# Gate and up products of a decoder layer on one NeuronCore: one weight sum as an accumulating transfer, a new order of the weight preparation, and six wide products in 17 blocks

## The chip, the core and the metric

The kernel runs on one core of one Trainium2 chip. The metric is the device time of one execution in microseconds (us); the figure of a kernel is the median of its runs. A profile is one further execution, recorded by the hardware profiler.

## The reference

The reference is one layer of a decoder in float32, with 512 tokens of width 1024: a mixer sublayer (causal stick-breaking attention beside a gated short convolution), cross-attention into 256 memory tokens, and a SwiGLU sublayer with 2816 hidden units, with a final norm. The change touches the first half of the last sublayer alone:

```python
hf = rms_norm(x, norm_ffn[l])
gate, up = jnp.split(hf @ w_ffn_in[l], 2, axis=-1)
x = x + (jax.nn.silu(gate) * up) @ w_ffn_out[l]
```

Here `hf` is 512 x 1024 and `w_ffn_in` is 1024 x 5632.

## The kernel before

**Precision.** TensorE works in a shortened float32 (`F32R`). Each operand is therefore split into a high part, which is a cast by ScalarE (`nc.scalar.copy`), and a rest, which is a subtraction on VectorE (`rest_of`, L1006). A product of two operands is three matmuls: high by high, high by rest, rest by high.

**Blocks and products.** The hidden units are worked in `NF` = 22 blocks of 128. A block needs a 1024 x 128 gate part and a 1024 x 128 up part of the weights. Pairs of row blocks of the activations against pairs of weight columns make 2 x 2 block products, and these are computed in a form that needs seven products instead of eight, of sums and differences of the operands. The tokens stand in two halves of `HS` = 256 columns. So a block has seven products, numbered 0 to 6, each over `KP` = 4 steps of 128 rows. The sums and differences of the activations (`forms_of`, L697) are made once, in the residual stage ahead. The activation forms of products 1, 2, 5 and 6 lie side by side, high half and rest half, in one tile of 512 columns (`both` in `product`); those of 3 and 4 are made the same way, but only their two halves are handed on.

**Narrow and wide products** (`product`, L899). A narrow product takes three matmuls of 256 columns per step, 12 in all, into the left half of a PSUM bank. A wide product takes, per step, one matmul of 512 columns (the weights' high part against both halves) and, after all four steps, one of 256 columns per step (the weights' rest against the high half): 4 and 4. The right half of its bank then holds a part that has to be added later. Products 1, 2 and 6 are wide in all blocks, product 5 in blocks 5 to 18 (`WIDE`, L921).

**Banks.** Products 0, 3, 4 and 5 of a block add up in one bank `z`, and ScalarE copies intermediate states out of it (`reads`, L939) to the tiles `s` and `t`. Product 1 goes to bank `v`. Products 2 and 6 add up in bank `y`. VectorE joins the two halves of a wide bank with an older state in two additions of 256 columns (`joined_halves`, L935): after product 1 and after product 6 for the gate, and in `second` for product 2. `evict` (L955) scales the gate, applies Silu on ScalarE and multiplies by the up part.

**The weights of a block.** Four quarters of 256 KB lie in HBM. `ffn_load` (L846) loads one quarter twice into `ws` and two quarters into `wg`, both through SP's queue, and then adds two quarters onto `ws` by an accumulating transfer of 512 KB through POOL's queue (L862). `sum_third` (L872) adds one half of `ws` onto `wg` on VectorE; `sum_last` (L876) adds the two halves of `wg` on VectorE and writes into the second half of a further tile `a22`, whose first half `load_corner` (L865) has filled with a quarter from HBM. `pair_cast` casts two forms at once: `wg` for products 0 and 1 (number 0), `ws` for products 4 and 2 (number 1), `a22` for products 5 and 6 (number 2). `third_cast` casts the form of product 3. Casts go to the tags `wh` and `wl`, four buffers each; `ws` and `wg` take turns over three blocks.

**The order.** PE, ScalarE and VectorE run a hand-written order. `uses` lists the products; from block 2 on the row of a block m is:

```python
uses += [(m, 3), (m, 2), (m, 4), (m + 1, 0), (m + 1, 1), (m, 5), (m, 6)]
```

The table `todo` (filled by `at` and `made`, L1076 and L1080) tells which casts, rests, sums and transfers are issued behind which product; `made` issues a cast at one place and its rest on VectorE at the next. ScalarE and VectorE work through their instructions in that order. SP and POOL only issue transfers here and are not in the manual order; each still issues its own in order.

Of the kernel before, what the change touches and what calls it, by code (L numbers as in the profile page):

```python
# [13 lines left out]
P = 128  # L14
# [12 lines left out]
HS = S // 2  # L27
# [17 lines left out]
def hybrid_layer(ctx: ExitStack, tc: tile.TileContext, xT_d, memT_d, mem_d, cols_d, wv_d, win_d,  # L45
# [653 lines left out]
    def forms_of(xe, xo):  # L699
# [144 lines left out]
    KP = KD // 2  # L844
    raws, corners = {}, {}

    def ffn_load(m):
# [4 lines left out]
        s13 = s13[0].tile([P, 2, 512], F32, tag=s13[1], name=nm("ws"))  # L852
        i = nc.sync.dma_start(s13, a[:, 2:3, :].broadcast_to([P, 2, 512]))
        if m < 2:
            after(i, [loads[-6]])
        wg = wg[0].tile([P, 2, 512], F32, tag=wg[1], name=nm("wg"))
        i = nc.sync.dma_start(wg, a[:, 0:2, :])
        if m < 2:
            after(i, [loads[-6]])
        if m < 2:  # L860
            load_corner(m)
        nc.gpsimd.dma_start(s13, a[:, 0:4:3, :], accum_op=ALU.add)  # L862
        raws[m] = wg, s13
# [12 lines left out]
    def sum_last(m, eng=nc.vector):  # L876
        wg = raws[m][0]
        eng.tensor_tensor(out=corners[m][:, 1, :], in0=wg[:, 0, :], in1=wg[:, 1, :], op=ALU.add)
# [22 lines left out]

    def product(ps, m, i, ks=range(KP)):

        rests = []
        for k in ks:
            hi, lo = (w[:, k * P:(k + 1) * P] for w in wforms[m, i])
            xh, xl, *both = x2f[k][i]
            if both and (i != 5 or m in WIDE):
                nc.tensor.matmul(ps, hi, both[0], start=i < 3 and k == 0, stop=False,  # L909
                                 skip_group_check=True)  # L910
                rests.append((ps[:, :HS], lo, xh))
                continue
            for j, (a, b) in enumerate(((hi, xh), (hi, xl), (lo, xh))):
                nc.tensor.matmul(ps[:, :HS], a, b, start=i < 3 and k == 0 and j == 0,  # L914
                                 stop=k == KP - 1 and j == 2, skip_group_check=True)
        for operands in rests:
            nc.tensor.matmul(*operands, start=False,  # L917
                             stop=ks[-1] == KP - 1 and operands is rests[-1],
                             skip_group_check=True)

    WIDE = range(5, NF - 3)  # L921
    banks, silus = {}, []
# [16 lines left out]
    def reads(m, i):  # L939

        b = banks[m]
        z, s, t = b["z"][:, :HS], b["s"], b["t"]
        if i == 5 and m in WIDE:
            nc.scalar.copy(s[:, :HS], b["z"][:, HS:])
        elif i in (0, 3, 4):
# [3 lines left out]
        elif i == 6:  # L949
            joined_halves(b["g"][:, HS:], b["y"], s[:, HS:])  # L950

    def second(m):
        b = banks[m]
        joined_halves(b["t"][:, HS:], b["y"], b["t"][:, :HS])

    def evict(m, part):
# [6 lines left out]
        else:  # L963
# [5 lines left out]
            if m in WIDE:  # L969
                first = b["s"][:, :HS]  # L970
                nc.vector.tensor_tensor(out=first, in0=b["z"][:, :HS], in1=first, op=ALU.add)
# [8 lines left out]
    uses = [(0, 0), (0, 1), (0, 2), (1, 0), (1, 1), (0, 3), (1, 3), (0, 4), (1, 2), (0, 5), (0, 6),  # L980
            (1, 4), (2, 0), (2, 1), (1, 5), (1, 6)]
    for m in range(2, NF - 1):
        uses += [(m, 3), (m, 2), (m, 4), (m + 1, 0), (m + 1, 1), (m, 5), (m, 6)]
    m = NF - 1
    uses[-1:] = [(m, 3), (m, 2), (m, 4), (m - 1, 6), (m, 5), (m, 6)]
# [153 lines left out]
    for m in range(NF - 2):  # L1139
        at(uses.index((m, 1)), lambda m=m: ffn_load(m + 2))  # L1140
    for m in range(1, NF - 1):
        p = {i: uses.index((m, i)) for i in range(2, 7)}
        q = {i: uses.index((m + 1, i)) for i in range(2)}
        if m > 1:
            at(p[3], lambda m=m: sum_third(m + 1))
# [4 lines left out]
            made(p[2], third_cast, m + 1)  # L1150
        else:
            made(p[4], third_cast, m + 1)
        at(p[4], lambda m=m: second(m))
        if m + 2 < NF:
            at(p[4], lambda m=m: load_corner(m + 2))
        made(q[0], pair_cast, m + 1, 1, late=2)
        at(q[1] if m < NF - 2 else p[4], lambda m=m: sum_last(m + 1))
        if m + 2 < NF:
            made(p[5], pair_cast, m + 2, 0)
# [34 lines left out]
    with tc.manual_schedule(engines={mybir.EngineType.PE, mybir.EngineType.Activation,  # L1194
# [6 lines left out]
        for n, (m, i) in enumerate(uses):  # L1201
            if n == 3:
                product(banks[m]["z"], m, i, range(KP - 1, KP))
            elif n > 3:
                product(bank_of(m, i), m, i)
# [329 lines left out]
```

## Time and profile before

| what | us |
|---|---|
| median of 3 runs | 839.65 |
| lowest and highest of them | 839.28, 840.1 |
| profiled execution | 838.75 |
| its span, first to last instruction | 837.0 |
| first to last product of gate and up | 502.4 to about 721 |

The profile page gives, per engine, busy time, share of the span and count of instructions. PE is TensorE's matmuls, PEld its weight loads, DVE VectorE, ACT ScalarE, POOL GpSimd, SP the engine that issues most transfers. A group of the page reads: line, engine, operation, written tile <- read tiles, shapes, count, then busy time and mean ns of one, then idle time of the engine just before, with what ended it. A row of the timeline reads: start from the span's beginning, length, engine, line, operation, tiles, shape, count of merged instructions. The length of a merged row of matmuls reaches to the end of the last one, which overlaps the next row, so the pace of PE is read from starts. A row on a queue of transfers reads: packets, MB, share of the 16 DMA engines. A row of issues ends in the median time from issue to landing.

### The profile page before, as it was taken

The page shows a single profiled execution, that of the slowest core. Times are in us where ns is not written, and L with a number is a line of the kernel's source. Part 1 is how long each engine was busy: PE and PEld are TensorE (multiplying, and loading weights), DVE is VectorE, ACT ScalarE, POOL GpSimd, SP SyncE. Part 2 cuts the span into 40 slices and gives each one's busy share as a digit, 9 for nine tenths or more (in the row PEclk, how much of TensorE's full clock was granted, in tenths as well). Part 3 has the DMA queues.
Part 4 walks back from the last instruction along what each step waited for, and adds up shares of the span by engine and source line. Part 5 has one row for each costly group of instructions (what it writes and reads, how often), then busy time and mean ns, then how long its engine had stood idle before and what let it go on. Part 6 is the DMA issues. An engine that isn't in the chain of part 4 may idle for free.

```text
span 837.0 us, 11962 instructions
## 1 busy us (share of the span) xinstructions
PE 828.8 (99%) x4374; PEld 714.1 (85%) x4374; DVE 684.6 (82%) x1086; ACT 463.9 (55%) x796; POOL 161.2 (19%) x168
## 2 busy tenths in 40 slices
PE   9999999999999999999999999999999999999996
PEld 7888888888888888888888789999999999888885
DVE  7879899996756576587555698999999999999886
ACT  7567868674332355434444566645555555576654
POOL 0011131110566630173000031111111110000401
PEclk9999999999999999999999999999999999999999
DMA  8552435235687865566431326677767673465552
GB/s 303 155 166 101 122 111 103 74 115 174 228 312 276 304 249 188 182 233 249 148 82 51 101 51 161 167 184 200 197 180 197 176 184 95 170 213 197 180 183 101
DMA packets 51357, 143.69 MB, mean 172 GB/s; under 512 B 5761, under 2 KB 7041, under 8 KB 48482
## 3 DMA queue, kind: packets, MB, share of 16 engines
q1 hardware_dynamic: 41650, 107.89, 38.2%
q0 software_dynamic: 9360, 34.75, 15.8%
q8 instruction: 34, 0.56, 0.3%
q10 hardware_dynamic: 288, 0.28, 0.1%
q14 instruction: 25, 0.20, 0.1%
HBM read 125.20 MB, written 13.64 MB: 166 GB/s over the span
## 4 chain that ended last, share of the span: by engine, by line
PE 99%; DVE 0%; ACT 0%; DVEq 0%; issue 0%
PE z L914 13%; PE p L1228 12%; PE pr L161 8%; PE pr L162 8%; PE pr L163 8%; PE y L909 5%; PE r L162 3%; PE r L163 3%; PE r L161 3%; PE v L288 3%; PE y L917 2%; PE v L909 2%; PE km L666 2%; PE mq L163 2%; PE mq L161 2%; PE mq L162 2%
## 5 line engine op out<-in xcount | busy, mean ns | idle before, releaser
L156 ACT CAST wh<-wr 128x1024 fp32r<-128x1024 f32 x84 | 88.0, 1051 | 144.2 <-issue 80.0
L157 DVE TENSOR_TENSOR wl<-wr,wh 128x1024 fp32r<-128x1024 f32 x84 | 111.0, 1321 | 32.0 <-ACT wh L156 31.9
L161 PE MATMUL pr<-xgh,wh 128*128 128x512 f32 x288 | 112.8, 392 | 0.0
L162 PE MATMUL pr<-xgl,wh 128*128 128x512 f32 x288 | 112.4, 390 | 0.0
L163 PE MATMUL pr<-xgh,wl 128*128 128x512 f32 x288 | 112.3, 390 | 0.0
L611 POOL TENSOR_TENSOR pre<-pre 128x512 f32<-128x512 f32 x44 | 70.9, 1616 | 31.5 <-DMA pre<-in_w_ffn_out_dram 29.2
L862 POOL DMA_DIRECT2D ws<-in_w_ffn_in_dram x22 | 26.6, 1209 | 248.5 <-DVE c L708 54.0
L163 PEld LDWEIGHTS pr<-xgh,wl 128*128 128x128 f32 x288 | 54.1, 188 | 11.5
L161 PEld LDWEIGHTS pr<-xgh,wh 128*128 128x128 f32 x288 | 54.1, 188 | 10.6
L162 PEld LDWEIGHTS pr<-xgl,wh 128*128 128x128 f32 x288 | 54.1, 188 | 10.5
L914 PE MATMUL z<-xd,wf 128*128 128x256 f32 x360 | 47.5, 282 | 0.0
L946 ACT COPY sa<-z 128x256 f32<-128x256 f32 x44 | 16.4, 373 | 51.9 <-PE z L914 51.9
L914 PEld LDWEIGHTS z<-xd,wf 128*128 128x128 f32 x360 | 45.0, 190 | 0.1
L1006 DVE TENSOR_TENSOR wf<-wg,wf 128x1024 fp32r<-128x1024 f32 (+1 forms) x44 | 43.1, 978 | 1.5
L1006 DVE TENSOR_TENSOR wl<-wr,wh 128x1024 fp32r<-128x1024 f32 x33 | 41.0, 1242 | 1.8 <-ACT wh L1073 1.8
L1073 ACT CAST wh<-wr 128x1024 fp32r<-128x1024 f32 x33 | 34.5, 1050 | 5.3 <-ACT f01h L1002 2.6
L914 PE MATMUL z<-xf,wf 128*128 128x256 f32 x264 | 35.4, 283 | 0.0
L914 PE MATMUL z<-xc,wf 128*128 128x256 f32 x264 | 35.1, 283 | 0.0
L914 PEld LDWEIGHTS z<-xf,wf 128*128 128x128 f32 x264 | 33.4, 192 | 0.1
L914 PEld LDWEIGHTS z<-xc,wf 128*128 128x128 f32 x264 | 33.0, 190 | 0.0
L368 DVE TENSOR_TENSOR g<-pr,r0b 128x512 f32<-128x512 f32 x16 | 11.0, 687 | 23.5 <-PE pr L163 23.5
L417 POOL TENSOR_SCALAR_AFFINE_SELECT e<-e 128x128 f32<-128x128 f32 (+1 forms) x24 | 10.7, 447 | 86.6 <-DVE e L470 86.6
(356 smaller groups left out, 2239.9 us busy)
## 6 DMA issues: line engine op xcount, KB each, us to landing
wr<-in_w_in_dram SPq DMA_DIRECT2D x36, 512.0 KB, 3.4
pre<-in_w_ffn_out_dram POOLq DMA_DIRECT2D x11, 1024.0 KB, 8.0
sums<-pre POOLq DMA_DIRECT2D x11, 1024.0 KB, 5.0
ws<-in_w_ffn_in_dram SPq DMA_DIRECT2D x22, 512.0 KB, 4.8
wg<-in_w_ffn_in_dram SPq DMA_DIRECT2D x22, 512.0 KB, 4.7
ws<-in_w_ffn_in_dram POOLq DMA_DIRECT2D x22, 512.0 KB, 5.7
wr<-sums SPq DMA_DIRECT2D x22, 512.0 KB, 4.0
wr<-in_w_ffn_out_dram SPq DMA_DIRECT2D x16, 512.0 KB, 3.7
```

The lines of the kernel that those rows point to most:

```text
L156: after(nc.scalar.copy(h2, raw), lead[-1:])
L157: lows.append(nc.vector.tensor_tensor(out=l2, in0=raw, in1=f(h2), op=ALU.subtract))
L161: nc.tensor.matmul(ps, a[0], b[0], start=start, stop=False, **kw)
L162: nc.tensor.matmul(ps, a[0], b[1], start=False, stop=False, **kw)
L163: nc.tensor.matmul(ps, a[1], b[0], start=False, stop=stop, **kw)
L611: nc.gpsimd.tensor_tensor(out=t[:, a, :], in0=t[:, a, :], in1=t[:, b, :], op=ALU.add)
L862: nc.gpsimd.dma_start(s13, a[:, 0:4:3, :], accum_op=ALU.add)
L909: nc.tensor.matmul(ps, hi, both[0], start=i < 3 and k == 0, stop=False, skip_group_check=True)
L914: nc.tensor.matmul(ps[:, :HS], a, b, start=i < 3 and k == 0 and j == 0, stop=k == KP - 1 and j == 2, skip_group_check=True)
L1006: nc.vector.tensor_tensor(out=lo, in0=src, in1=f(hi), op=ALU.subtract)
L1073: nc.scalar.copy(hi, raw)
L1228: nc.tensor.matmul(res[i][s2], a[:, ts], b, start=j == 0 and n == 0, stop=n == 2 and j == (BEHIND - 1 if (i, s2) == (5, 1) else NJ - 1))
```

## The change

1. Products 3 and 4 hand on their 512-column tiles, and in blocks 3 to 19 (the new `WIDE`, 17 blocks) products 3, 4 and 5 are wide beside 1, 2 and 6. Only product 0 stays narrow there. ScalarE copies all 512 columns of bank `z` after products 3 and 4, and VectorE folds them in with one addition of 512 and one of 256 columns (`folded`) in place of two of 256.
2. Products 5 and 6 of these blocks run as a pair: the eight matmuls of 512 columns of both, then the eight of 256 columns (`beside_next`, `later`).
3. In blocks 4 to 20 (`OWN`) the last sum is no longer VectorE's: POOL issues an accumulating transfer of 256 KB from the first half of `wg` onto its second half. The corner quarter is then loaded over that first half, and `pair_cast` number 2 reads `wg`; `a22` isn't used in these blocks.
4. The order around it moves: the sum of the third form stands behind product 5 of the block two ahead, followed by the accumulating transfer; the third form's cast and the cast for products 0 and 1 come a product earlier; the loads into `ws` are issued earlier than those into `wg`; the corner's load stands behind product 2 of the preceding block.

```diff
-        return [(u[:, a], u[:, b]), first, second, third[:2], fourth[:2], fifth, last]
+        return [(u[:, a], u[:, b]), first, second, third, fourth, fifth, last]
...
+    OWN = range(4, NF - 1)
...
+            after(nc.gpsimd.dma_start(s13, a[:, 0:4:3, :], accum_op=ALU.add), own_sums[-1:])
 
     def load_corner(m):
 
+        if m in OWN:
+            nc.sync.dma_start(raws[m][0][:, 0, :], wfi_d[m][:, 3 * 512:])
+            return
...
     def sum_last(m, eng=nc.vector):
         wg = raws[m][0]
+        if m in OWN:
+            own_sums.append(nc.gpsimd.dma_start(wg[:, 1, :], wg[:, 0, :], accum_op=ALU.add))
+            return
...
-        raw = (*raws[m], corners[m])[which]
+        raw = (*raws[m], raws[m][0] if m in OWN else corners[m])[which]
...
-            if both and (i != 5 or m in WIDE):
+            if both and (i not in (3, 4, 5) or m in WIDE):
...
-    WIDE = range(5, NF - 3)
+        if later:
+            return ends
+        ends()
+
+    WIDE = range(3, NF - 2)
...
-        if i == 5 and m in WIDE:
-            nc.scalar.copy(s[:, :HS], b["z"][:, HS:])
+        if m in WIDE and i in (3, 4):
+            nc.scalar.copy((s, t)[i - 3], b["z"])
+        elif m in WIDE and i == 5:
+            nc.scalar.copy(t[:, :HS], b["z"][:, HS:])
+        elif m in WIDE and i == 6:
+            folded(b["g"][:, HS:], b["y"], s)
...
+    def folded(out_, bank, old):
+        nc.vector.tensor_tensor(out=old, in0=bank, in1=old, op=ALU.add)
+        nc.vector.tensor_tensor(out=out_, in0=old[:, :HS], in1=old[:, HS:], op=ALU.add)
+
     def second(m):
         b = banks[m]
+        if m in WIDE:
+            folded(b["t"][:, HS:], b["y"], b["t"])
+            return
...
+        if m + 2 in OWN:
+            made(q[1], pair_cast, m + 2, 0)
+            at(p[5], lambda m=m: sum_third(m + 2), lambda m=m: sum_last(m + 2))
...
+            elif (m, i) in beside_next:
+                ends = [product(bank_of(*use), *use, later=True) for use in uses[n:n + 2]]
+                ends[0]()
```

In the rows below, each instruction stands with its line, operation, written tile, read tiles and columns; numbers behind names tell buffers apart.

On PE, product 3 of block 5 before, with the start of product 2 behind it (`z_5351` is the block's bank z, `xd` the activation form, `wf` the weights):

```order
L914 MATMUL z_5351<-xd_4436,wf_5331 128x256 x3
L914 MATMUL z_5351<-xd_4537,wf_5331 128x256 x3
L914 MATMUL z_5351<-xd_4638,wf_5331 128x256 x3
L914 MATMUL z_5351<-xd_4739,wf_5331 128x256 x3
L909 MATMUL y_5435<-xc_4430,wf_5369 128x512
```

The same product of the same block now (its bank z is `z_5332`):

```order
L922 MATMUL z_5332<-xd_4436,wf_5302 128x512
L922 MATMUL z_5332<-xd_4537,wf_5302 128x512
L922 MATMUL z_5332<-xd_4638,wf_5302 128x512
L922 MATMUL z_5332<-xd_4739,wf_5302 128x512
L932 MATMUL z_5332<-xd_4436,wf_5302 128x256
L932 MATMUL z_5332<-xd_4537,wf_5302 128x256
L932 MATMUL z_5332<-xd_4638,wf_5302 128x256
L932 MATMUL z_5332<-xd_4739,wf_5302 128x256
```

Twelve matmuls of 256 columns became four of 512 and four of 256.

On PE, product 5 of block 5 and the start of product 6 before (`y_5435` is its bank y):

```order
L909 MATMUL z_5351<-xd_4439,wf_5432 128x512
L909 MATMUL z_5351<-xd_4540,wf_5432 128x512
L909 MATMUL z_5351<-xd_4641,wf_5432 128x512
L909 MATMUL z_5351<-xd_4742,wf_5432 128x512
L917 MATMUL z_5351<-xd_4439,wf_5433 128x256
L917 MATMUL z_5351<-xd_4540,wf_5433 128x256
L917 MATMUL z_5351<-xd_4641,wf_5433 128x256
L917 MATMUL z_5351<-xd_4742,wf_5433 128x256
L909 MATMUL y_5435<-xo_4442,wf_5432 128x512
```

The same place now (bank y is `y_5412`):

```order
L922 MATMUL z_5332<-xd_4439,wf_5409 128x512
L922 MATMUL z_5332<-xd_4540,wf_5409 128x512
L922 MATMUL z_5332<-xd_4641,wf_5409 128x512
L922 MATMUL z_5332<-xd_4742,wf_5409 128x512
L922 MATMUL y_5412<-xo_4442,wf_5409 128x512
L922 MATMUL y_5412<-xo_4543,wf_5409 128x512
L922 MATMUL y_5412<-xo_4644,wf_5409 128x512
L922 MATMUL y_5412<-xo_4745,wf_5409 128x512
L932 MATMUL z_5332<-xd_4439,wf_5410 128x256
```

Product 6 begins ahead of the second half of product 5, four matmuls of 256 columns earlier.

On VectorE, from the join of product 1 of block 9 to the end of block 8's row before (`wg_5617` and `ws_5615` are block 9's, `wg_5733` and `ws_5731` block 10's, `fg_5720` is block 8's gate):

```order
L937 TENSOR_TENSOR fg_5833<-v_5832,fg_5833 128x256
L878 TENSOR_TENSOR a_5692<-wg_5617 128x512
L1006 TENSOR_TENSOR wf_5830<-ws_5615,wf_5829 128x1024
L936 TENSOR_TENSOR fg_5720<-y_5779,sa_5695 128x256
L937 TENSOR_TENSOR fg_5720<-y_5779,fg_5720 128x256
L1006 TENSOR_TENSOR wf_5861<-wg_5733,wf_5860 128x1024
L874 TENSOR_TENSOR wg_5733<-ws_5731,wg_5733 128x512
L960 TENSOR_TENSOR fg_5720<-fg_5720,r0b_4940 128x512
L1006 TENSOR_TENSOR wf_5890<-a_5692,wf_5889 128x1024
L1006 TENSOR_TENSOR wf_5903<-wg_5733,wf_5903 128x512
```

The same place now (`ws_5510` is block 9's, `ws_5614` and `wg_5684` are block 10's, `fg_5673` is block 8's gate):

```order
L956 TENSOR_TENSOR fg_5777<-v_5776,fg_5777 128x256
L1039 TENSOR_TENSOR wf_5774<-ws_5510,wf_5773 128x1024
L1039 TENSOR_TENSOR wf_5791<-wg_5684,wf_5790 128x1024
L884 TENSOR_TENSOR wg_5684<-ws_5614,wg_5684 128x512
L976 TENSOR_TENSOR sa_5648<-y_5730,sa_5648 128x512
L977 TENSOR_TENSOR fg_5673<-sa_5648 128x256
L990 TENSOR_TENSOR fg_5673<-fg_5673,r0b_4940 128x512
L1039 TENSOR_TENSOR wf_5828<-wg_5684,wf_5828 128x512
L1039 TENSOR_TENSOR wf_5832<-wg_5577,wf_5831 128x1024
L976 TENSOR_TENSOR sb_5756<-y_5834,sb_5756 128x512
```

The L878 sum is gone, and the rest for products 0 and 1 and the sum of the third form stand ahead of the reads of product 6 instead of behind them.

More of the change, by code (lines that the diff above doesn't have):

```diff
@@ L845, in hybrid_layer, with ffn_load @@
     raws, corners = {}, {}
-    def ffn_load(m):
+    OWN = range(4, NF - 1)
+    own_sums = []
+    def ffn_load(m, which=("s", "g")):
         a = wfi_d[m].rearrange("p (i c) -> p i c", i=4)
@@ L900, in third_cast, with product @@
         return one_form(m, 3, *((fpool, "wg") if m == NF - 1 else (wpool, ("wh", "wl")[m % 2])))
-    def product(ps, m, i, ks=range(KP)):
+    def product(ps, m, i, ks=range(KP), later=False):
         rests = []
@@ L915, in product, with ends @@
                                  stop=k == KP - 1 and j == 2, skip_group_check=True)
[L916 to L919, printed above, removed]
-    WIDE = range(5, NF - 3)
+        def ends():
+            for operands in rests:
+                nc.tensor.matmul(*operands, start=False,
+                                 stop=ks[-1] == KP - 1 and operands is rests[-1],
+                                 skip_group_check=True)
+        if later:
+            return ends
+        ends()
+    WIDE = range(3, NF - 2)
     banks, silus = {}, []
@@ L981, in hybrid_layer @@
             (1, 4), (2, 0), (2, 1), (1, 5), (1, 6)]
+    beside_next = set()
     for m in range(2, NF - 1):
         uses += [(m, 3), (m, 2), (m, 4), (m + 1, 0), (m + 1, 1), (m, 5), (m, 6)]
+        if m in WIDE:
+            beside_next.add((m, 5))
     m = NF - 1
@@ L1149, in hybrid_layer @@
             made(p[3], pair_cast, m, 2)
-            made(p[2], third_cast, m + 1)
+            if m + 1 not in OWN:
+                made(p[2], third_cast, m + 1)
         else:
```

46 lines of the change are left out of this document (30 added, 16 removed).

## The prediction

> **What bounds the kernel now.** The page comes first: its span, the engines' shares, the chain of work that ended last.
>
> ```profile
> span 837.0 us, 11962 instructions
> PE 828.8 (99%) x4374; PEld 714.1 (85%) x4374; DVE 684.6 (82%) x1086; ACT 463.9 (55%) x796; POOL 161.2 (19%) x168
> PE 99%; DVE 0%; ACT 0%; DVEq 0%; issue 0%
> ```
>
> TensorE is the chain, end to end. A long busy time alone proves little, since matmuls are pipelined; so next the stretch that the change touches (the gate and up products), in one row of the table of stretches. Its columns are length, then busy time of PE, PEld, DVE, ACT and POOL, the granted clock, the DMA share and GB/s.
>
> ```profile
> 560.00:700.00 140.00, 140.00 (x964) 130.16 (x963) 135.52 (x234) 75.87 (x128) 16.86 (x14) 1.00 0.69 182
> ```
>
> PE is covered for all 140 us at full clock, and VectorE is close behind with 135.52. Whether PE has hidden gaps is seen from the starts in the timeline (start, length, ..., count). The first two rows open two successive blocks, of which the earlier has all of products 3, 4 and 5 narrow; from 565.31 on stands one whole block with wide product 5, in the order of the program: products 3, 2, 4, then 0 and 1 of the next block, 5, 6.
>
> ```profile
> 545.45 1.59 PE L914 MATMUL z<-xd,wf 128*128 128x256 f32 x12
> ...
> 555.39 1.59 PE L914 MATMUL z<-xd,wf 128*128 128x256 f32 x12
> ...
> 565.31 1.60 PE L914 MATMUL z<-xd,wf 128*128 128x256 f32 x12
> 566.74 1.09 PE L909 MATMUL y<-xc,wf 128*128 128x512 f32 x4
> 567.67 0.63 PE L917 MATMUL y<-xc,wf 128*128 128x256 f32 x4
> 568.14 1.59 PE L914 MATMUL z<-xc,wf 128*128 128x256 f32 x12
> 569.57 1.60 PE L914 MATMUL z<-xf,wf 128*128 128x256 f32 x12
> 571.01 1.09 PE L909 MATMUL v<-xo,wf 128*128 128x512 f32 x4
> 571.94 0.63 PE L917 MATMUL v<-xo,wf 128*128 128x256 f32 x4
> 572.41 1.09 PE L909 MATMUL z<-xd,wf 128*128 128x512 f32 x4
> 573.34 0.64 PE L917 MATMUL z<-xd,wf 128*128 128x256 f32 x4
> 573.82 1.09 PE L909 MATMUL y<-xo,wf 128*128 128x512 f32 x4
> 574.75 0.63 PE L917 MATMUL y<-xo,wf 128*128 128x256 f32 x4
> 575.22 1.59 PE L914 MATMUL z<-xd,wf 128*128 128x256 f32 x12
> ```
>
> Starts follow each other without a gap. A narrow product (12 matmuls of 256 columns) takes 1.43 us (565.31 to 566.74) and a wide one (4 of 512, 4 of 256) 1.40 (566.74 to 568.14), 1.41 for product 5. So PE is bound by its own instructions: the change can win only what it takes from them, and can lose whatever it makes PE wait.
>
> **The change part by part. PE.** The columns streamed stay the same: 3 x 256 against 512 + 256 per step. Only the price of each instruction goes: 1.43 / 12 = 0.119 us for 256 columns, 0.93 / 4 = 0.233 for 512 (571.01 to 571.94), so 0.358 against 0.351 a step. The blocks with six wide products are 3 to 19; products 3, 4 and 5 of 17 blocks are 51, of which 14 (product 5 of blocks 5 to 18) are wide already: 37 products become wide, each worth 0.02 (by 1.41) to 0.03 (by 1.40). Product 0 stays narrow; after a narrow one it takes 1.44 (569.57 to 571.01), and it will now follow a wide one as the 1.43 ones do: up to 0.01 in 17 blocks.
>
> The Trainium skill ("TensorE: Matmul & The Clock Gate", Back-to-back issue gap) gives N / 2.4 + 2.5 ns between matmuls: 109 ns at 256 columns and 216 at 512, so 2.5 ns saved a step, and 37 x 4 x 2.5 = 0.4 us in all. The trace disagrees, with 119 and 233 ns.
>
> The pair (both products' 512s, then all eight 256s) has a likeness in the memory keys, which run 8 and 8:
>
> ```profile
> 302.61 2.00 PE L666 MATMUL km<-mg,wh 128*128 128x512 f32 x8
> 304.45 1.12 PE L669 MATMUL km<-mg,wl 128*128 128x256 f32 x8
> 305.41 0.86 PE L666 MATMUL km<-mg,wh 128*128 128x512 f32 x3
> ```
>
> From 302.61 to 305.41 it is 2.80 us; products 5 and 6 take 2.81 now (572.41 to 575.22). The pair is worth 0 to 0.02 a block; I take 0.01.
>
> A block goes from 9.91 (565.31 to 575.22) to about 9.83: 0.06 for products 3 and 4, 0.01 for product 0, 0.01 for the pair. A block with narrow product 5 goes from 9.94 (545.45 to 555.39) to 9.83. Sum: 14 x 0.08 + 3 x 0.11 = 1.45, rounded to **1.4 us off PE**. The ends: 37 x 0.02 = 0.75, and 37 x 0.03 + 17 x 0.01 + 17 x 0.02 = 1.6.
>
> **VectorE** loses one sum and gets wider reads. Its rows in the next block:
>
> ```profile
> 575.42 0.42 DVE L936 TENSOR_TENSOR fg<-y,sa 128x256 f32<-128x256 f32 x1
> 575.88 0.42 DVE L937 TENSOR_TENSOR fg<-y,fg 128x256 f32<-128x256 f32 x1
> 576.22 1.22 DVE L1006 TENSOR_TENSOR wf<-wg,wf 128x1024 fp32r<-128x1024 f32 x1
> 577.47 0.69 DVE L874 TENSOR_TENSOR wg<-ws,wg 128x512 f32<-128x512 f32 x1
> 578.08 0.68 DVE L960 TENSOR_TENSOR fg<-fg,r0b 128x512 f32<-128x512 f32 x1
> 578.68 1.22 DVE L1006 TENSOR_TENSOR wf<-a,wf 128x1024 fp32r<-128x1024 f32 x1
> ...
> 581.37 0.41 DVE L971 TENSOR_TENSOR sa<-z,sa 128x256 f32<-128x256 f32 x1
> ...
> 583.75 0.68 DVE L878 TENSOR_TENSOR a<-wg 128x512 f32<-128x512 f32 x1
> 584.35 1.22 DVE L1006 TENSOR_TENSOR wf<-ws,wf 128x1024 fp32r<-128x1024 f32 x1
> ```
>
> The sum at L878 goes in 17 blocks: 0.60 each (583.75 to 584.35). Two joins a block, 0.80 each now (575.42 to 576.22), become one add of 512 and one of 256 that needs it: 0.60 (as L960, 578.08 to 578.68) to 0.69, plus 0.34 (575.88 to 576.22), so 0.95 to 1.05, and 0.3 to 0.5 more for the two. Blocks 3, 4 and 19 also get the add at L971 (0.45). VectorE ends 0.1 to 0.3 lighter in most blocks; none of it is on the path.
>
> The limits for PE: product 6 may not write bank y before VectorE has read product 2 from it (that join is the instruction ahead of L971: done at 581.37, 6.15 into the block). PE wanted it at 8.51 (573.82 - 565.31); the pair wants it at 9.83 - 2.80 + 0.93 = 7.96. The fold is at most 0.25 longer than a join, with a 0.60 sum gone ahead of it, so some 2 us are left. Less is left where the order changes over, ahead of block 3: there VectorE takes on the next block's third sum a product earlier (L874, 0.61), and a wait at that place costs up to 0.6 once. In bank z, ScalarE must have copied product 4 before product 5. That copy grows:
>
> ```profile
> L946 ACT COPY sa<-z 128x256 f32<-128x256 f32 x28 | 10.4, 373 | 33.4 <-PE z L914 33.4
> L962 ACT ACTIVATE fg<-fg 128x512 f32<-128x512 f32 x14 | 8.9, 633 | 9.5 <-DVE fg L960 9.5
> ```
>
> It goes from 0.37 to about 0.63 (the nearest 512-wide ScalarE row), twice a block: 0.5 us more on an engine that is busy 75.87 of 140, two products ahead of need. I cost it at nothing; uncovered it would be 0.26 a block, 4.4 in all.
>
> **The transfers.** The sum becomes an accumulating transfer of 256 KB inside wg, issued by POOL; the corner then lands where its source lay, so that load must wait for the sum, and the next wg load stands behind it on SP. The trace has no such transfer; the nearest are these: POOL's DMA queue over the same 140 us, its transfers into ws, and the times to landing of all into ws and of the corner loads (256 KB, plain).
>
> ```profile
> q0 software_dynamic: 3808, 7.34, 31.7%
> ws<-in_w_ffn_in_dram POOLq DMA_DIRECT2D x14, 512.0 KB, 5.7
> DMA to landing us min/median/max: 3.9/5.5/7.4
> DMA to landing us min/median/max: 2.4/2.5/5.1
> ```
>
> The sum is bounded by the fastest plain load of its size (2.4) and the slowest transfer into ws (7.4). I take 5.0, near the accumulating row's 5.7 with half its bytes; the corner takes 2.5, at most 5.1. Together 7.5, at most 12.5. The chain begins when VectorE has summed the third form. That ends now 2.86 into the following block (578.08 - 575.22); without the L878 sum and the join ahead of it, 1.46, so 11.3 after a block's start. It must end where the corner pair is cast, two blocks after that start, behind product 3, its copy and the third form's cast (1.40 and twice about 0.63): 19.66 + 2.66 = 22.3. That leaves 11.0 us for 7.5. PE itself needs the pair at product 5, 4 us later. So I cost the chain at nothing. DMA load: 14 transfers of 512 KB were 31.7% of 140 us, 3.2 us each; half of that per 9.83 adds 0.16 to a share of 0.69. It rises to 0.85, below full, but queues lengthen.
>
> The Trainium skill ("DMA: Bandwidth & Descriptors", Two DMAs through the same engine are not ordered) says that only the first transfer's full semaphore allows the second: sum and corner can't overlap. The chain above is reckoned that way.
>
> **The rivals.** *The chain ties up VectorE (slower).* Behind the corner load VectorE works in order: the pair's rest (1.25, 576.22 to 577.47), the fold (1.0), the last reads of a block (L971 and three of 256, 1.6), the join of product 1 (0.8), two rests (2.5) and the next third sum (0.6), 7.8, after a cast of at most 1.3. Two blocks (19.66) less 9.1 leave 10.6 for both transfers: from there on VectorE falls back by half the excess in every block, and once its 2 us are used up PE waits for it before product 6. At 12.5 this is 0.95 a block, for some 14 blocks 13, less 1.4: 851; at 11.6, 0.5 a block, 7 less 1.4: 845. For it speaks the share of 0.85; against it, that each transfer would have to take nearly its longest time, in every block.
>
> *The 512s run faster when they come in longer rows.* Inside the keys' run (302.61 to 304.45) eight take 1.84, 0.230 each against 0.233: nothing more than reckoned. If the rate fell to 0.227, six products of four would win 0.14 a block, 2.4 in all, and the kernel would gain 3.8: 835.9.
>
> *The saving is only that of the fixed cost of a matmul*, 2.5 ns a step or 0.4 us: 839.25. This is the page's rule on gaps, above. Against it stand 14 blocks in which product 5 already is wide and the block 0.03 shorter.
>
> *Some blocks wait*, at the first wide block or once at the last: 0.5 to 1 of the 1.4 comes back, and the result is no change, 839.0.
>
> **How the numbers follow.** The profiled execution took 838.75 (span 837.0); the three runs have a median of 839.65, 0.9 above it. The sum takes 1.4 from either: 837.35 for a profiled run, **838.25** for a median. About 0.2%, 1.7 us, is what a measurement of this kernel can tell from no change, and the forecast lies just inside.
>
> Chances: forecast 0.66, the chain 0.10, longer rows 0.06, fixed cost only 0.10, some waits 0.08. The forecast's ends (0.75 to 1.6) with 0.4 us of scatter (the runs lie from 839.28 to 840.1) give 837.65 to 839.3; a good fifth of it lies beyond 1.7 us. Faster: 0.06 + 0.15 = 0.21. Same: 0.51 + 0.10 + 0.08 = 0.69. Slower: 0.10. The range, 837.5 to 840.0, takes in the forecast, fixed cost only and some waits, and leaves out the chain and most of the longer rows.
>
> **What would show it.** Right: a block of 9.83 between starts of product 3, 1.40 for products 3 and 4, 2.80 for the pair, PE still at 140 of 140, the new transfers landing within 7.4, VectorE under 135.5. Wrong: gaps between PE starts ahead of product 5 or 6, casts on ScalarE waiting for a transfer into wg, or a block shorter than 9.80.

## The result: slower by 1.1%, and the profile after

| | median us | runs | profiled execution | its span |
|---|---|---|---|---|
| before | 839.52 | 6, 839.28 to 840.1 | 838.75 | 837.0 |
| after | 847.35 | 6, 844.5 to 855.3 | 846.79 | 844.7 |

The ratio is 1.011, with a 95% interval of 1.0067 to 1.0153. The runs after lie 11 us apart, those before less than 1: the time now hangs on something that comes out differently from run to run.

From the page, the chain that ended last.

```profile
PE 85%; DVE 8%; DMA 4%; issue 1%; ACT 1%; DVEq 0%; ACTq 0%; SPq 0%; POOLq 0%
```

PE was 99% of the chain; now VectorE and the DMA have 12% of it. The gate and up stretch, columns as in the prediction:

```profile
560.00:700.00 140.00, 134.97 (x810) 119.68 (x809) 128.87 (x212) 78.74 (x122) 27.41 (x26) 0.99 0.82 196
```

PE lacks 5.0 of its 140 us, and the DMA share is 0.82 for the 0.85 expected (0.89 in e2 below, where PE does not wait). Where the 5.0 lie and what ended them, from the table of waits of 500 to 735 us (total, times, longest):

```profile
PE z L922 <- ACT sb L963: 5.0, 2, 3.1
PE y L932 <- DVE wf L1039: 0.7, 1, 0.7
```

Two waits, both ahead of product 5, both for ScalarE's copy of product 4 out of bank z (L963). The timeline shows the first, ScalarE's rows and PE's:

```profile
616.70 0.62 ACT L908 CAST wf<-wg 128x512 fp32r<-128x512 f32 x1
...
621.19 0.63 PE L932 MATMUL v<-xo,wf 128*128 128x256 f32 x4
622.77 1.05 ACT L900 CAST wf<-wg 128x1024 fp32r<-128x1024 f32 x1 [5.45 <-DMA wg<-in_w_ffn_in_dram]
623.72 0.62 ACT L992 ACTIVATE fg<-fg 128x512 f32<-128x512 f32 x1
...
624.25 0.56 ACT L963 COPY sb<-z 128x512 f32<-128x512 f32 x1
...
624.87 1.18 PE L922 MATMUL z<-xd,wf 128*128 128x512 f32 x4 [3.05 <-ACT sb L963]
```

The cast of the corner pair (L900) waits 5.45 us for the corner load, which itself takes 6.2 us from its issue, by the row of the chain in order of time (start, length, what):

```profile
616.52 6.17 DMA wg<-in_w_ffn_in_dram
```

Ahead of this row the chain runs on through VectorE's rows, though SP's table of waits puts the issue at 616.52 down to the sum transfer; so the 8% of VectorE need not be VectorE's own. Behind the cast on ScalarE, in order, stand the silu (L992) and the copy of product 4. PE has finished product 4 long ago and has run products 0 and 1 of the next block; it stops at 621.66 (621.19 and the 0.47 us between two such starts), since product 5 may not overwrite its bank.

The second wait costs more than it shows:

```profile
674.07 0.63 PE L932 MATMUL v<-xo,wf 128*128 128x256 f32 x4
676.66 1.20 PE L922 MATMUL z<-xd,wf 128*128 128x512 f32 x4 [1.95 <-ACT sb L963]
677.70 1.62 PE L922 MATMUL y<-xo,wf 128*128 128x512 f32 x4
679.11 1.06 PE L932 MATMUL z<-xd,wf 128*128 128x256 f32 x4
...
680.83 1.38 PE L922 MATMUL z<-xd,wf 128*128 128x512 f32 x4
682.05 0.64 PE L932 MATMUL z<-xd,wf 128*128 128x256 f32 x4
```

Behind the gap four 512s take 1.41 us (677.70 to 679.11) instead of 0.93, the two times four 256s 1.72 (679.11 to 680.83) instead of 0.94, and the next 512s 1.22: TensorE ran at about half its pace for some 3 us, 0.48 + 0.78 + 0.29 = 1.55 us more. The granted clock over 678.04 to 681.45 is 0.50; it is 1.00 before and behind. The gaps are 3.21 (621.66 to 624.87) and 2.12 (674.54 to 676.66). With the 1.55 and the 0.7 at L932 it is 7.6; less about 1.3 that the wide products save (below), 6.3 of the 7.7 us of span between the profiles. Of the other 1.4, 0.4 lies ahead of the gate and up products (the first starts at 502.75 instead of 502.38); the rest is spread over small delays that I have not followed.

### The profile page after: what moved, and what is told of

The parts are those of the page before. It is cut to its first block, busy times and chain, and to the rows that moved or that the text cites. A ratio compares the mean times of both kernels' runs of the same rounds, so it can differ in the third digit from the quotient of the medians.

```text
span 844.7 us, 11683 instructions
## 1 busy us (share of the span) xinstructions
PE 830.7 (98%) x4226; PEld 707.6 (84%) x4226; DVE 682.9 (81%) x1072; ACT 472.5 (56%) x799; POOL 175.5 (21%) x185
## 4 chain that ended last, share of the span: by engine, by line
PE 85%; DVE 8%; DMA 4%; issue 1%; ACT 1%; DVEq 0%; ACTq 0%; SPq 0%; POOLq 0%
PE p L1279 12%; PE pr L161 8%; PE pr L162 8%; PE pr L163 8%; DVE wf L1039 4%; PE z L927 4%; PE r L163 3%; PE r L161 3%; PE r L162 3%; PE v L288 3%; PE y L922 2%; PE z L922 2%; DMA wg<-in_w_ffn_in_dram 2%; DMA wg<-wg 2%; PE km L666 2%; PE mq L163 2%
## 5 line engine op out<-in xcount | busy, mean ns | idle before, releaser
L1039 DVE TENSOR_TENSOR wf<-wg,wf 128x1024 fp32r<-128x1024 f32 (+1 forms) x61 | 62.8, 1045 | 10.5 <-ACT wf L900 10.2
L870 POOL DMA_DIRECT2D ws<-in_w_ffn_in_dram x22 | 26.6, 1210 | 187.0 <-DMA ws<-in_w_ffn_in_dram 74.6
L162 PEld LDWEIGHTS pr<-xgl,wh 128*128 128x128 f32 x288 | 54.1, 188 | 10.5
L900 ACT CAST wf<-wg 128x1024 fp32r<-128x1024 f32 x39 | 41.0, 1052 | 14.9 <-DMA wg<-in_w_ffn_in_dram 13.1
L922 PE MATMUL z<-xd,wf 128*128 128x512 f32 x136 | 37.8, 399 | 5.0 <-ACT sb L963 5.0
L922 PEld LDWEIGHTS z<-xd,wf 128*128 128x128 f32 x136 | 23.5, 191 | 8.9 <-ACT sb L963 5.7
L889 POOL DMA_DIRECT2D wg<-wg x17 | 15.9, 934 | 59.3 <-ACT sa L963 30.0
L1039 DVE TENSOR_TENSOR wf<-ws,wf 128x1024 fp32r<-128x1024 f32 (+1 forms) x23 | 26.9, 1169 | 0.0
```

Of the source, the lines that this page charges most:

```text
L162: nc.tensor.matmul(ps, a[0], b[1], start=False, stop=False, **kw)
L1039: nc.vector.tensor_tensor(out=lo, in0=src, in1=f(hi), op=ALU.subtract)
```

## Why the corner load was late, as the trace shows it

The transfers of the same stretch, median us to landing (before: 5.7, 2.5, and no third):

```profile
ws<-in_w_ffn_in_dram POOLq DMA_DIRECT2D x13, 512.0 KB, 8.5
...
wg<-in_w_ffn_in_dram SPq DMA_DIRECT2D x13, 256.0 KB, 3.5
wg<-wg POOLq DMA_DIRECT2D x13, 256.0 KB, 7.0
```

The sum transfer (`wg<-wg`, L889) was taken at 5.0 and takes 7.0. The issues of POOL and SP in order of time show why. On POOL, L870 is the accumulating load into `ws` and L889 the sum; on SP, L875 is the corner load, L863 the wg load, L857 the plain load into `ws` on which the next L870 builds.

```profile
561.01 1.20 POOL L870 DMA_DIRECT2D ws<-in_w_ffn_in_dram  x1 [1.89 <-DMA ws<-in_w_ffn_in_dram]
...
568.18 0.90 POOL L889 DMA_DIRECT2D wg<-wg  x1 [5.97 <-DVE wg L884]
...
604.11 0.33 SPq L875 DMA_DIRECT2D wg<-in_w_ffn_in_dram  x1
604.54 0.37 SPq L863 DMA_DIRECT2D wg<-in_w_ffn_in_dram  x1
604.77 1.20 POOL L870 DMA_DIRECT2D ws<-in_w_ffn_in_dram  x1 [6.71 <-DMA ws<-in_w_ffn_in_dram]
605.01 0.38 SPq L857 DMA_DIRECT2D ws<-in_w_ffn_in_dram  x1
607.12 0.90 POOL L889 DMA_DIRECT2D wg<-wg  x1 [1.14 <-ACT sa L963]
...
616.52 0.33 SPq L875 DMA_DIRECT2D wg<-in_w_ffn_in_dram  x1
616.63 0.90 POOL L889 DMA_DIRECT2D wg<-wg  x1 [1.78 <-DVE wg L884]
...
617.43 0.73 SPq L857 DMA_DIRECT2D ws<-in_w_ffn_in_dram  x1
...
626.86 1.20 POOL L870 DMA_DIRECT2D ws<-in_w_ffn_in_dram  x1 [9.33 <-DMA ws<-in_w_ffn_in_dram]
```

At 568 the accumulating load leads the sum by 7.17 us. At 607 it leads by 2.35 (604.77 to 607.12), and the sum lands, as the corner load's issue tells, at about 616.5: 9.4 us after its issue. The sum stands behind the accumulating load in POOL's DMA queue. The two transfers of that turn (KB, us to landing):

```profile
ws<-in_w_ffn_in_dram POOLq DMA_DIRECT2D x1, 512.0 KB, 10.4
...
wg<-wg POOLq DMA_DIRECT2D x1, 256.0 KB, 9.3
```

The load is issued at 604.77 and lands at 615.1, the sum 1.3 later; from 545 to 705 no sum lands ahead of the load before it. And the three loads of SP now leave in one bunch, because the corner load at the head of that queue waits for the sum (126.9 us of waiting in all from 545 to 730, by the table of SP's waits). So there is a loop: accumulating load (604.77), sum behind it, landed by 616.52, then the `ws` load behind the corner load (617.43), then the accumulating load that builds on it, which waits for it until 626.86 (one more, at 613.65, belongs to the block between). That is 22.1 us for two blocks, while PE, left alone, runs two in 19.7 (twice the 9.84 of e3, below). The lead shrinks from turn to turn until the corner is too late and PE waits; the wait gives the lead back (5.21 at 632), and it shrinks again (1.33 at 661). The loop isn't closed from the start: up to 585 the `ws` load leaves 2.1 to 3.7 us behind the wg load, when its buffer comes free, and the lead falls no lower than 5.7, where it falls in e3 and e11 (below) too. From 594.76 on the `ws` load leaves right behind the corner load, and the leads that follow are 3.96, 2.35 and 2.98.

This is the theory that the runs have to test: **the loop** through the two queues. Its rivals: **load** (more traffic makes every transfer late), **length** (the chain of sum, corner load and cast is too long whatever stands in the queues), and **wide reads** (the 512-wide copies and folds of ScalarE and VectorE are the cost).

## The experiments

Medians, each beside the kernel before run with it on the same chip:

| run | edit, against the changed kernel | us | before | ratio, 95% |
|---|---|---|---|---|
| e1 | no sum transfers | 838.52 | 839.43 | 0.9979 to 0.9997 |
| e2 | transfers of the same size, nobody waits | 838.32 | 839.43 | 0.9977 to 0.9996 |
| e3 | corner in its own tile | 838.24 | 839.43 | 0.9974 to 0.9993 |
| e4 | sum on VectorE | 846.68 | 839.43 | 1.0069 to 1.0102 |
| e5 | products narrow | 846.68 | 839.59 | 1.0061 to 1.0097 |
| e6 | corner load behind wg load | 847.8 | 839.59 | 1.008 to 1.012 |
| e7 | corner load on POOL | 850.0 | 839.59 | 1.0109 to 1.0157 |
| e8 | pair's cast later | 851.29 | 839.59 | 1.0126 to 1.0156 |
| e9 | sum ahead of the accumulating load | 838.71 | 840.03 | 0.9976 to 0.9995 |
| e10 | e3, sum behind that load | 856.86 (one run) | 840.03 | |
| e11 | corner load on ScalarE | 840.33 | 839.71 | 1.0001 to 1.0021 |

### Is it the transfer, its load, or its chain (e1, e2, e3)

e1:

```diff
-            own_sums.append(nc.gpsimd.dma_start(wg[:, 1, :], wg[:, 0, :], accum_op=ALU.add))
```

> The changed kernel without its 17 sum transfers (leaves the last sum of the weights out in blocks 4 to 20); the corner load still lands in the weight tile and waits only for the third form's rest. Chain of transfers (sum, corner load, cast, copy) as the cause: the 8 us of waits go, what is left is TensorE's own gain, 838.2 (837.5 to 839). The load on the DMA engines as the cause: the same, since the load goes with the sum (share near 0.69). Wide copies and folds on ScalarE and VectorE as the cause: they are all still there, so 845 or more.

e2:

```diff
-            own_sums.append(nc.gpsimd.dma_start(wg[:, 1, :], wg[:, 0, :], accum_op=ALU.add))
+            own_sums.append(nc.gpsimd.dma_start(aside[0][:, 0, :], raws[m][1][:, 0, :],
+                                                accum_op=ALU.add))
```

> Each sum transfer is replaced by an accumulating transfer of the same size from the first weight tile into a tile that nobody reads (leaves the last sum of the weights out in blocks 4 to 20): the same load on the DMA engines, but nobody waits for it. Chain as the cause: 838 to 839.5, although the share of the DMA engines stays near 0.82. Load as the cause: the weight loads are late in any case, and TensorE waits in two to five blocks, 845 or more.

e3:

```diff
-        if m in OWN:
-            nc.sync.dma_start(raws[m][0][:, 0, :], wfi_d[m][:, 3 * 512:])
-            return
...
-        nc.scalar.copy(hi, raw)
+        if which == 2 and m in OWN:
+            raw = raw[:, 0, :], raws[m][0][:, 1, :]
+            for n in range(2):
+                nc.scalar.copy(hi[:, n, :], raw[n])
```

> The corner goes back to a tile of its own, loaded two blocks ahead, so that no load waits for the sum transfer and nothing stands behind such a load on SyncE; the sum transfer stays where it was (into the weight tile), and the cast and the rest of this pair are made in two halves (0.2 more on ScalarE, nothing more than 0.1 on VectorE in a block). Chain or the queue behind the waiting load as the cause: 838 to 840. Load as the cause: 845 or more, with waits for loads in place of those for the sum.

All three are at 838.2 to 838.5; e1 and e2 leave out a sum that the result needs. The stretch from 560 to 700 us of e2 (e3 has the same 140.00, 1.00 and 0.89):

```profile
560.00:700.00 140.00, 140.00 (x859) 125.05 (x858) 136.34 (x222) 83.18 (x130) 29.56 (x28) 1.00 0.89 211
```

The DMA engines are busier (0.89) than in the changed kernel (0.82), and PE is covered: load falls. The wide copies and folds are all there: wide reads fall too, as far as the transfer takes the sum off VectorE. What is left is a wait *for* the transfer. e3 computes everything, with the same sum transfer at the same place, and is 1.2 us faster than before. One block of it in PE's timeline:

```profile
585.42 1.09 PE L924 MATMUL z<-xd,wf 128*128 128x512 f32 x4
...
586.82 1.09 PE L924 MATMUL y<-xc,wf 128*128 128x512 f32 x4
...
589.62 1.59 PE L929 MATMUL z<-xf,wf 128*128 128x256 f32 x12
591.06 1.09 PE L924 MATMUL v<-xo,wf 128*128 128x512 f32 x4
...
592.46 1.09 PE L924 MATMUL z<-xd,wf 128*128 128x512 f32 x4
...
595.26 1.09 PE L924 MATMUL z<-xd,wf 128*128 128x512 f32 x4
```

9.84 a block (585.42 to 595.26), a wide product 1.40, product 0 1.44, the pair 2.80. And its sum transfer:

```profile
wg<-wg POOLq DMA_DIRECT2D x14, 256.0 KB, 4.4
```

The same sum takes 4.4 instead of 7.0, although the engines are busier.

### What the wide products are without the transfer, and the transfer without them (e4, e5)

e4:

```diff
-    OWN = range(4, NF - 1)
+    OWN = range(0)
```

> Only the wide products and the pair; the sum stays on VectorE and the weights are prepared as before. If VectorE has room (9.5 us busy in a block before, 0.3 to 0.5 more now, against a block of 9.83): 838.2. If it has none: it takes 9.9 to 10.0 a block, TensorE waits for it before product 6, and the time is 839 to 842.

The direction was open, and the size is above the 839 to 842 expected: 846.68. VectorE's timeline, at the fold of product 2 of one block and of the block two later, and a sum between:

```profile
572.99 0.68 DVE L976 TENSOR_TENSOR sb<-y,sb 128x512 f32<-128x512 f32 x1
...
575.97 0.68 DVE L891 TENSOR_TENSOR a<-wg 128x512 f32<-128x512 f32 x1
576.57 1.22 DVE L1039 TENSOR_TENSOR wf<-ws,wf 128x1024 fp32r<-128x1024 f32 x1
...
593.74 0.68 DVE L976 TENSOR_TENSOR sb<-y,sb 128x512 f32<-128x512 f32 x1
```

Two blocks take 20.75 us, 10.38 each, and VectorE's instructions follow each other with no gap over 0.1 us between: it is the bound, 0.54 above the 9.84 of PE, in 17 blocks 9.2 (8.4 measured beyond e3). Without the sum (0.60, 575.97 to 576.57) it would be at 9.78. So the wide products need the sum off VectorE, and by this estimate it has 0.06 us a block left even then.

e5:

```diff
-    WIDE = range(3, NF - 2)
+    WIDE = range(0)
```

> The sum transfers and the corner load that waits for them, as changed, but products 3, 4 and 5 narrow in all blocks and no pair. VectorE has about 0.6 us a block less to do than in the kernel before, but its place in the chain is set by the casts, so the sum starts no earlier. Chain of transfers as the cause: TensorE waits as in the changed kernel, and without its gain of 1.4: 845 to 856. Wide reads as a part of the cause (they delay the third sum, and so the start of the chain): no waits, 839.5 to 841.

846.68 (844.1 to 847.43): the waits come with light reads as well. VectorE is at 120.24 of 140 here:

```profile
560.00:700.00 140.00, 138.01 (x988) 130.27 (x987) 120.24 (x198) 68.05 (x109) 28.63 (x27) 0.99 0.82 201
```

So neither VectorE's load nor the wide reads make the chain late. In the profile, which is of the fastest of the four runs, the lead of the accumulating load over the sum falls from 7.0 (561 to 568 us) to 1.5 (666 to 668) in ten blocks, and then PE waits once, 2.0 us.

### Where in the queues (e6, e7, e8)

e6:

```diff
-                at(p[2], lambda m=m: load_corner(m + 1))
+                at(q[1], lambda m=m: load_corner(m + 1))
```

> The corner load is issued by SyncE behind the load of the next weight tile instead of ahead of it. If the queue behind the waiting corner load makes the transfers slow (the other loads leave in a bunch, the transfer into the sum's other half runs late, and the next sum queues behind it): the load that is now ahead is free, the bunch is two instead of three, and the time falls by some us, 839 to 846. If it is only the length of the chain: the corner comes no earlier, 845 to 856 as it was.

847.8 (846.01 to 850.27): no better, which by its own expectation speaks for length. The wg load is no longer held and lands in 5.9 instead of 7.1, but the `ws` load, which feeds the accumulating load, still stands behind the corner load (8.2 to landing, as before the edit). So it buys nothing to free the wg load while the `ws` load is held; this run alone can't tell loop from length.

e7:

```diff
-            nc.sync.dma_start(raws[m][0][:, 0, :], wfi_d[m][:, 3 * 512:])
+            own_sums.append(nc.gpsimd.dma_start(raws[m][0][:, 0, :], wfi_d[m][:, 3 * 512:]))
...
-            at(uses.index((m - 1, 3)), lambda m=m: ffn_load(m + 2, "s"))
...
                 at(p[2], lambda m=m: load_corner(m + 1))
+                if m + 3 in OWN:
+                    at(p[2], lambda m=m: ffn_load(m + 3, "s"))
```

> The corner load is issued by GpSimd ahead of the accumulating load of the same block instead of by SyncE, so that SyncE's loads wait for no sum, and the accumulating load for the block after comes behind the corner in GpSimd's queue; the chain of sum, corner load and cast stays. If the chain is too long by itself: 845 or more. If it is too long only because the waiting load holds SyncE's queue: the sum lands within about 4.5 us and the corner within about 3.5, 8 of the 10.2 us between the sum's issue and the cast; no waits, 838 to 839.5.

850.0 (849.0 to 853.25), which by its own expectation speaks for length. But the edit put another loop in the place of the first, on POOL's queue alone:

```profile
597.65 1.23 POOL L870 DMA_DIRECT2D ws<-in_w_ffn_in_dram  x1
601.26 0.89 POOL L889 DMA_DIRECT2D wg<-wg  x1 [2.38 <-issue]
608.66 0.57 POOL L875 DMA_DIRECT2D wg<-in_w_ffn_in_dram  x1 [6.51 <-DVE fg L956]
609.22 1.24 POOL L870 DMA_DIRECT2D ws<-in_w_ffn_in_dram  x1
```

The accumulating load now stands behind the corner load, which waits for the sum, which stands behind the accumulating load before: 11.57 us round (597.65 to 609.22). It comes round in every block; the turns from 554.98 to 695.25 take 9.65 to 11.57 us, 10.8 in the mean with PE's waits in them, for 9.84 of work. The run was no fair test.

e8:

```diff
-            made(p[3], pair_cast, m, 2)
+            made(p[4] if m in OWN else p[3], pair_cast, m, 2)
```

> The cast of the corner pair is moved behind ScalarE's copy of product 4 (and its rest on VectorE one product later) in the 17 blocks; the transfers stay as changed. If ScalarE's order (the copy and the silu stand behind a cast that waits) carries the wait to TensorE: the chain has about 3 us more, 838 to 841. If transfers are late whatever waits for them and pile up: 843 or more, with TensorE waiting for the pair's weights themselves.

851.29 (851.09 to 852.01), in the range given for transfers that are late whatever waits for them. The waits for ScalarE's copy are gone and two of 0.9 for the cast itself are left, but its rest on VectorE now comes just when the pair's 256s need it. The weight loads of PE wait there 14 times, 9.0 us in all, and two blocks take 20.79 (565.09 to 585.88) instead of 19.68. One of these waits:

```profile
585.88 0.74 PE L932 MATMUL z<-xd,wf 128*128 128x256 f32 x4 [0.51 <-DVE wf L1039]
```

So moving the cast only changes the place at which the late pair reaches PE, and costs a wait in nearly every block. It gives no answer on loop against length.

### The order in POOL's queue (e9, e10)

e9:

```diff
-        if "s" in which:
-            after(nc.gpsimd.dma_start(s13, a[:, 0:4:3, :], accum_op=ALU.add), own_sums[-1:])
+        if which == ("s", "g"):
+            second_half(m)
...
             at(p[5], lambda m=m: sum_third(m + 2), lambda m=m: sum_last(m + 2))
+            if m > 2 and m + 3 in OWN:
+                at(p[5], lambda m=m: second_half(m + 3))
```

where `second_half` is that accumulating load alone.

> Of the two transfers that GpSimd issues in a block, the sum now goes ahead of the accumulating load of the next tile (512 KB) instead of behind it; everything else as changed, the chain and SyncE's queue included. If the sum is late because it stands behind that load in GpSimd's DMA queue: it lands in 4.4 to 5.5 us, the corner 2.5 to 3.5 later, 8 of the 10.2 us, and TensorE does not wait: 838 to 839.5. If the chain is too long without that, or the load on the DMA engines makes it so: the sum still takes 7 and the time is 845 or more. A new wait could come from the accumulating load itself, which starts up to 3 us later and is needed by the next third sum on VectorE.

838.71 (838.2 to 839.15), 9 us less, with the chain, SP's queue and the in-place corner untouched. POOL's rows and the transfers:

```profile
607.83 0.90 POOL L893 DMA_DIRECT2D wg<-wg  x1 [7.83 <-ACT sa L967]
608.39 1.58 POOL L874 DMA_DIRECT2D ws<-in_w_ffn_in_dram  x1
```

```profile
ws<-in_w_ffn_in_dram POOLq DMA_DIRECT2D x15, 512.0 KB, 6.5
...
wg<-in_w_ffn_in_dram SPq DMA_DIRECT2D x14, 256.0 KB, 3.9
wg<-wg POOLq DMA_DIRECT2D x14, 256.0 KB, 4.0
```

The sum takes 4.0, the corner 3.9, 7.9 of the 10.2 us between the sum's issue and the cast (607.12 to 617.3 in the changed kernel, the end of L908 at 616.70 + 0.62). The length is not too long, once nothing stands ahead of the sum.

e10, on top of e3:

```diff
+    def late_sum(m):
+        sum_last(m)
+        after(own_sums[-1], adds[-1:])
...
+            at(uses.index((m - 1, 3)), lambda m=m: late_sum(m))
```

> The corner apart again (no load waits for the sum), but in 15 blocks the sum goes behind the next accumulating load in GpSimd's DMA queue: the opposite order, where nobody is waiting. If the place in the queue sets the sum's time: 7 us or more from issue to landing against 4.4, in a kernel in which TensorE waits for nothing, 838 to 839. If the bunch of loads behind a waiting corner sets it: it stays at 4 to 5.5.

The transfer's time came out as the queue has it, in a kernel in which no load waits for the sum and SP's loads don't bunch:

```profile
wg<-wg POOLq DMA_DIRECT2D x13, 256.0 KB, 8.7
```

8.7 against 4.4 in e3; the 15 sums land 0.8 to 2.5 us after the accumulating load that went 0.7 to 0.9 ahead of them. The time, 856.86 in one run, was missed by 18 us: I had thought that nobody waits for the sum there, but the pair's cast reads its result a block later, and PE waited in most blocks.

The Trainium skill ("DMA: Bandwidth & Descriptors", Two DMAs through the same engine are not ordered) says that within one queue of one engine descriptors start in order but are pipelined. The runs agree as far as they show it: in e10 each delayed sum lands behind the load ahead of it, and soon after.

### The loop through SP alone (e11)

```diff
-            nc.sync.dma_start(raws[m][0][:, 0, :], wfi_d[m][:, 3 * 512:])
+            nc.scalar.dma_start(raws[m][0][:, 0, :], wfi_d[m][:, 3 * 512:])
...
-                at(p[2], lambda m=m: load_corner(m + 1))
...
+    for m in OWN:
+        at(uses.index((m, 1)), lambda m=m: load_corner(m))
```

> The corner load is issued by ScalarE, behind its last cast of a block, instead of by SyncE; GpSimd's order of the sum and the accumulating load and the chain of sum, corner load and cast stay. In the changed kernel the accumulating load is issued 7.3 us ahead of the sum at first, then 5.7, 4.0 and 2.4, until TensorE waits. If that slip is a loop through SyncE's queue (late sum, late corner load, late weight loads behind it, late accumulating load, later sum): the loop is cut, the lead stays at 5 us or more, the sum takes 4 to 5.3, 838 to 839.5. If the chain by itself, or the order in GpSimd's queue by itself, is too long: the lead shrinks as before, ScalarE now waits at the load, and the time is 845 or more.

840.33 (838.73 to 841.88). POOL's program is that of the changed kernel; only SP no longer waits. In the profiled execution (838.73) PE is covered for all 140 us. Its corner load and sum:

```profile
wg<-in_w_ffn_in_dram ACTq DMA_DIRECT2D x14, 256.0 KB, 5.3
wg<-wg POOLq DMA_DIRECT2D x14, 256.0 KB, 4.6
```

The lead stays between 4.9 and 7.0 us from 558 to 697 (5.2 to 7.4 in e3), the sum takes 4.6, where the changed kernel had 7.0. So the slip is the loop through SP. The median lies 0.8 above the range expected of that, and the runs 3 apart: the corner load leaves later here and takes 5.3, and ScalarE's cast waits for it ten times, 7.3 us in all, longest 1.9. I take that as what is left of the length, but the longer runs have no profile, so it isn't shown. Against the kernel before, the changed kernel stands at +7.8, e11 at +0.6 and e3 at -1.2: of the 9.0 us lost, the loop through SP has 7.2, and about 1.8 stays in e11. That a corner has to follow the sum is no cost by itself, since it does so in e9 too, which stands at -1.3.

## Why the prediction was wrong, step by step

- **PE's gain: right, a little large.** 1.4 was forecast. A block is 9.84, not 9.83: products 3 and 4 gain the 0.03 each, the pair 0.01, product 0 nothing (1.44). 14 x 0.07 + 3 x 0.10 = 1.28, and e2, e3 and e9 are 1.1 to 1.3 under the kernel before. The rival *fixed cost only* (0.4) and *longer rows* (3.8) fall with it.
- **VectorE: the terms were right, at the upper end.** A fold is 0.25 longer than a join (in e4, between starts, 0.71 for L976 and 0.34 for L977, against 0.80), the upper bound given; so VectorE ends as heavy as before, not 0.1 to 0.3 lighter (e2: 136.34 in 140 / 9.84 blocks, 9.58 each; before 135.52 in 140 / 9.91, 9.59). But the 2 us that the prediction saw at the read of product 2 are no room for more work in each block: e4 shows 0.06 a block to spare with the sum gone, and -0.54 with it.
- **The transfers: this step failed.** "The sum is bounded by the fastest plain load of its size (2.4) and the slowest transfer into ws (7.4). I take 5.0": it took 7.0 in the median and 9.4 at 607. Alone it is 4.0 (e9), so 5.0 was no bad price for a transfer by itself. What was missing is what stands ahead of it in its own queue. The corner was 3.5 for 2.5. In the medians that is 10.5 of a window of 10.2, where I had 7.5 of 11.0. In the turn that stops PE the two take 9.4 and 6.2: from the sum's issue to the cast it is 15.65 (607.12 to 622.77), and the 5.45 beyond the 10.2 are the wait in the profile. So the step "So I cost the chain at nothing" is the one that fails: the median is 7.8 us longer, not 1.4 shorter. Two of the prediction's own signs of being wrong show it: gaps ahead of product 5, and a cast on ScalarE that waits for a transfer into wg.
- **The queue on SP: named and not followed.** The prediction says that the next load stands behind the corner load. It doesn't follow the `ws` load behind that, to the accumulating load that waits for it, and from there to the next sum. A step was priced once, which comes round again every two blocks with the delay of the turn before.
- **"PE itself needs the pair at product 5, 4 us later": wrong as cover.** The cast of the pair is followed on ScalarE by the copy that frees bank z, so a late pair stops PE through the copy (L963).
- **The rival *the chain ties up VectorE*** had the place, a point of decision of 10.6 us for both transfers (measured 10.5) and a price of 845 to 851, in which the result lies. That is luck: by its own rule transfers of 10.5 would have cost nothing. Its carrier was wrong: e5 loses as much with VectorE at 120 of 140. The carrier is ScalarE's order. Its chance, 0.10, was argued from "each transfer would have to take nearly its longest time, in every block"; the loop drives the sum there, turn by turn.

Two versions beat both kernels: e3 (838.24, ratio 0.9984, 0.9974 to 0.9993) and e9 (838.71, 0.9986, 0.9976 to 0.9995). They keep the change's wide products and its sum transfer, and cut the loop at one place each.

## What to carry to other kernels

Price a new transfer by what stands ahead of it in its own queue, not by transfers of its size alone; and where a load is made to wait, follow every load behind it until the path ends or comes back to its start. If it comes back, compare the time round with the time that the loop's work takes: here a turn of 22.1 us for 19.7 of work is hidden at first and stops PE some blocks later. (That the place differs from run to run is what the spread of 11 us suggests; only one of the runs has a profile.) When work moves off a nearly full engine to free it, try each half of the change alone: here the wide products without the transfer (e4) and the transfer without them (e5) lose 7 us each, and together, with the loop cut, they win 1.2.

## What was not expected of the hardware

The gap of 2.12 us in the matmuls at 674 was followed by 3.4 us at a granted clock of 0.50 (678.04 to 681.45), in which four 512s took 1.41 us for 0.93. Gaps of 2.15 (e5, at 673), 2.44 (e8, at 719), 3.02 (e7, at 636) and 2.42 and 2.84 (e10, at 673 and 618) were followed by 3.4 us at 0.50 as well, and in e6 one of 3.03 (at 632) by 6.8 and one of 3.94 (at 687) by 3.4. The low clock begins between 0.7 us ahead of the gap's end and 1.4 behind it. The gap of 3.21 at 621 was not, nor e7's of 2.18 at 614, nor any of the gaps of 1.0 to 1.5 in e7, e8 and e10. The Trainium skill ("TensorE: Matmul & The Clock Gate", HAM oscillation — how this bites in real kernels) warns of gaps above about 3.4 us; by these runs 2.1 can be enough, and 3.2 need not be.

An accumulating transfer of 256 KB from one half of a tile to the other takes 4.0 us to landing with nothing ahead of it (e9), and 8.7 behind a 512 KB one on the same queue (e10), at DMA shares of 0.86 and 0.80: the place in the queue counts for more than the load.
